# Projection stage of a two-layer hybrid trunk: when the deferred transposes and the splits of the gated outputs are written

## The chip, the cores and the metric

One NeuronCore of a Trainium2 chip runs the whole program in one launch. The metric is the device time in microseconds (us), the median of several executions. Engines are named as in the profile: PE (TensorE, with PEld for its weight loads), DVE (VectorE), ACT (ScalarE), POOL (GpSimd) and SP (SyncE, which issues most DMAs).

## The reference

Two identical layers work on 512 latent tokens and 128 context tokens of width 1024. The context tokens read themselves, the latent tokens read the context cache and all latent tokens.

```
h = rmsnorm(x) * (1 + sc1) + sh1
lru_x, lru_g, gq, gk, gv, dq, dk, dv = split(h @ w_in)      # 256,256,512,128,128,256,256,256 columns
lru_out = gelu(lru_g) * (forward scan + backward scan of the gated recurrence on conv4(lru_x))
gqa_out = softmax attention, 8 query heads on 2 key heads, per-head rmsnorm of q and k, 2-D rotary
d_out   = rmsnorm(softmax(q1 k1) v - lam * softmax(q2 k2) v), 4 heads
x = x + g1 * (concat(lru_out, gqa_out, d_out) @ w_out)
h = rmsnorm(x) * (1 + sc2) + sh2
x = x + g2 * ((silu(g) * a) @ w_down),   a, g = split(conv3(h @ w_up))
```

After the second layer comes one more rmsnorm. The keys, values and scan states of the context tokens are outputs as well.

## The kernel before, in words

Every large product is done in three passes of float32r matmuls: each operand is split into a rounded high part and the rest, and `mm3` (L342 to L346) adds high x high, high x low and low x high. A weight block of 128x1024 comes by a DMA on SP's queue, ACT writes its high part (L329) and DVE its low part (L330).

A layer has these stages in PE's order. The LRU columns m = 0, 1 come first, then three projection groups (`proj_group`, L604): gq, then gk, gv and dq together (`evac_kvdq`), then dk and dv (`evac_dkdv`). Each group has four steps c over the five token tiles, and a tile's result leaves PSUM in the last of them. Then come the LRU's gate columns m = 2, 3 (L1121 to L1125), `wait("a")`, a change of the PSUM pools (`psum_mode(3, 2)`, L1127), attention, the output projection (`out_proj`) and the ConvFFN (`ffn`).

Under the matmuls of the projection stage lies a lot of small work that belongs to attention: norms of the heads, rotary, rounding to high and low parts, and transposes on PE. One such stack for queries: POOL rounds (`s2b`), DVE subtracts (`s3`), PE transposes four blocks (`s4`, tile qT, L844), ACT copies twice. For grouped keys it is `k_stack` (tile kT), for differential keys `d_stack` and `d_stack_flow` (tile dT, whose result DVE copies, L914). The context block has its own small attention: `ctx_stage` (scores cS), `ctx_norm` (DVE), `ctx_T` (transposes cPTp).

Every engine runs its instructions in the order in which the program writes them, and this order comes from a small planner that runs while the program is written, `Flow`. It has a clock `now`. After each pair of k blocks the loops call `fl.step(ns)` with the time that they take the pair to need on PE. Work that has to come later is queued with `fl.add(delay, fn, dve, need)` and written at the first step whose time is past its due time. So a delay of 5000 means a place in program order some steps later, and an instruction written too early waits on its engine with everything behind it. `dve` is the time that `fn` will need on DVE: `fl.dve` is the planner's DVE clock, it moves by these times and by `fl.busy`, and work that has such a time is held back while this clock is over 1500 ns (`slack`) ahead of `now`. `need` names a resource: there are two "st" slots for all stacks. Some functions move `now` themselves, for their own transposes (`fl.now += 230`).

```
def add(self, delay, fn, dve=0.0, need=None):
    self.seq += 1
    self.items.append([self.now + delay, self.seq, fn, dve, need])
```

The gated LRU outputs are made in `lru_in` for m = 2, 3: ACT writes gelu, 800 later DVE multiplies (`mul`, L686), 800 later `mix_out` takes one of 22 buffers of the pool "halves", ACT rounds into it (L639), and DVE writes the rest 800 after that (L640). h itself lies in eight buffers of the same pool.

Between stages, `norm_pipe(t)` turns a finished token tile into h. `a`, 1250 after the tile's last residual, writes the sum of squares on ACT, the root and the two scaled halves xn on POOL (L543). `b`, 4000 (NP[1]) after that, writes eight transposes on PE (tile nT, L549) and the modulation on DVE and ACT. `hi` and `lo` follow 950 and 1700 later. It runs in the last token loops of `tok_products`, where a tile has four pairs of k blocks in the output projection and three in the last part of the FFN. During attention a second planner (`Plan`) sets the order and steps `Flow` by 20 ns.

Of the kernel before, what the change touches and what calls it, by code (L numbers as in the profile page):

```python
# [34 lines left out]
CX = (3000, 6500, 4000, 3000, 6000, 12000, 8000)  # L35
# [10 lines left out]
DT = 1500  # L46
# [8 lines left out]
class Flow:  # L55
# [7 lines left out]
    def add(self, delay, fn, dve=0.0, need=None):  # L63
        self.seq += 1
        self.items.append([self.now + delay, self.seq, fn, dve, need])

# [146 lines left out]
def hybrid_kernel(ctx: ExitStack, tc: tile.TileContext, i, o):  # L213
# [100 lines left out]
    def split_next():  # L314
        if pos[1] >= len(parts):
            return
        n, kind, b = parts[pos[1]]
        pos[1] += 1
        load_to(n)
        if kind == "a":  # L320
            split_done.append(n)
            return
        raw = raws[n][:, :, b * 128:b * 128 + 128] if kind == "c" else raws[n][:, 2 * b:2 * b + 2, :]
        if kind == "h":
            wh, wl = (half(nm, F32R)[:, 0:1024].rearrange("p (a b) -> p a b", a=2) for nm in ("wh", "wl"))
        else:
            wh = whp.tile(list(raw.shape), F32R, tag="wh", name="wh")
            wl = wlp.tile(list(raw.shape), F32R, tag="wl", name="wl")
        act.activation(out=wh, in_=raw, func=ACTF.Copy)  # L329
        dve.tensor_tensor(out=wl, in0=raw, in1=f32(wh), op=ALU.subtract)  # L330
        fl.busy(1130)
        split_done.append((wh, wl))
        if all(m != n for m, _, _ in parts[pos[1]:pos[1] + 3]):
            load_to(n + 2)
# [256 lines left out]
    def stat_mm(acc, w, hh, hl, c, n0=0, n1=KD):  # L591

        wh, wl = w
        for k in range(n0, n1):
            c0, c1 = (0, acc[2]) if c == 0 else (acc[2], T)
            cs = slice(c0, c1)
            mm3(acc[c][:, 0:c1 - c0], wh[:, k, :], wl[:, k, :],
                hh[k // 2][:, k % 2, cs], hl[k // 2][:, k % 2, cs], k == 0, k == KD - 1)
            if k % 2:
                fl.step(816)  # L600
# [12 lines left out]
    def proj_group(hh, hl, evac):  # L613
        acc = tok_acc("acc")
        for c in range(4):
            wh, wl = weights()
            for t in range(NT):
# [7 lines left out]
                fl.step(1296)  # L625


    def mixer(l, hh, hl, first=None):
# [15 lines left out]
        kr, pending = [], {"t": 0.0, "lru": 2, "a": 17}  # L644

        def lru_in(m, acc):
# [33 lines left out]
            else:  # L680
# [4 lines left out]
                def mul():  # L685
                    dve.tensor_tensor(out=gg, in0=gg, in1=lru["S"][:, c], op=ALU.mult)  # L686
                    fl.add(800, lambda: mix_out(c, gg))
# [15 lines left out]
        def lru_tail(c):  # L703
# [33 lines left out]
            fl.add(LT[0], lambda: s1(0), 1500)  # L737
            fl.add(LT[1], lambda: s1(1), 1500)
            fl.add(LT[2], s2)
            fl.add(LT[3], lambda: s3(0), 1700)  # L740
            fl.add(LT[4], lambda: s3(1), 1700)
# [66 lines left out]
        def evac_gq(t, a):  # L808
# [5 lines left out]
            def s1():  # L814
                got["r"] = head_rstd(n, 8)
                if t < 4:
                    fl.add(GQ[1], s2, 2700)
# [3 lines left out]
            def s2():  # L821
                scale_heads(n, got["r"], 8)
                rope(n, t, rope_t["q"], 8, 64)
                for g in range(2):
                    fl.add(100, lambda g=g: s2b(g), 0, "st")

            def s2b(g):
# [3 lines left out]
                fl.add(GQ[2], lambda: s3(g, st), 350)  # L831

            def s3(g, st):
                hs = slice(4 * g, 4 * g + 4)
                dve.tensor_tensor(out=st[:, :, 1 - g], in0=n3[:, hs], in1=f32(st[:, :, g]), op=ALU.subtract)
                fl.add(GQ[3], lambda: s4(g, st))
# [16 lines left out]
            def c2():  # L853
                scale_heads(n, got["r"], 8)
                dve.tensor_tensor(out=n3, in0=n3, in1=rope_t["qg"].unsqueeze(1).to_broadcast([128, 8, 64]), op=ALU.mult)
                fl.add(2500, c3)
# [10 lines left out]
        def k_stack(kf, c0):  # L867
# [6 lines left out]
            def lo():  # L874
                dve.tensor_tensor(out=st[:, 256:384].rearrange("p (h d) -> p h d", d=64), in0=k3, in1=f32(sh[:, :, 0]),
                                  op=ALU.subtract)
                fl.add(1300, tr)
# [14 lines left out]
            fl.add(2000, lo, 200)  # L892
# [27 lines left out]
        def d_stack_flow(lag, *args):  # L920
            lo, tr, out = d_stack(*args)

            def b():
                lo()
                fl.add(lag, c)
# [10 lines left out]
            fl.add(lag, b, 200)  # L936
# [20 lines left out]
        def evac_kvdq(t, a):  # L957
# [16 lines left out]
            def s1():  # L974
                got["r"] = head_rstd(n, 2)
                fl.add(2500, s2 if t < 4 else c2, 1000, "st" if t < 4 else None)

            def s2():
# [3 lines left out]
                fl.add(500, lambda: rope(dqt[:, t], t, rope_t["dq"], 8, 32), 1300)  # L982

            def c2():
# [5 lines left out]
                fl.add(2000, c3)  # L990
# [14 lines left out]
        def evac_dkdv(t, a):  # L1005
            act.activation(out=dv(t if t < 4 else 5), in_=a[:, 256:512], func=ACTF.Copy)
            if t < 4:
                act.activation(out=dkt[:, t], in_=a[:, 0:256], func=ACTF.Copy)
                fl.add(800, lambda: rope(dkt[:, t], t, rope_t["dk"], 8, 32), 1300)
# [34 lines left out]
        def ctx_stage(n):  # L1044
# [7 lines left out]
            fl.add(CX[2], lambda: ctx_norm(n), 900)  # L1052

        def ctx_norm(n):
# [9 lines left out]
            fl.add(CX[3], lambda: ctx_T(n))  # L1064

        def ctx_T(n):
            P = ctxP[n][0]
# [51 lines left out]
        for args in stack_args(0, "k"):  # L1119
            fl.add(CX[4], lambda args=args: d_stack_flow(1500, *args), 0, "st")  # L1120
# [5 lines left out]
        wait("a")  # L1126
        psum_mode(3, 2)  # L1127
# [163 lines left out]
    def tok_products(nk, stat, done, last=4):  # L1291
# [7 lines left out]
        for c in range((nk - last) // 2):  # L1299
            w = weights()  # L1300
            for t in range(NT):
                mms(t, 2 * c, w)
                mms(t, 2 * c + 1, w)
                fl.step(1296)
        ws = []
        for t in range(NT):
            for k in range(nk - last, nk):
# [4 lines left out]
                if k % 2 and k < nk - 1:  # L1312
                    fl.step(1296)
            done(t, acc(t))
            fl.step(1296)
# [331 lines left out]
```

## Time and profile before

| | |
|---|---|
| median of 3 executions | 1642.95 us (1642.11 to 1643.48) |
| the profiled execution | 1643.37 us, of which the span of its instructions is 1641.6 us |
| mean granted TensorE clock | 0.995 of full speed |
| PE busy | 1594.2 us, 97% of the span |
| DVE, ACT, POOL busy | 945.0, 726.3, 344.8 us |

The span is cut by stages: layer 0's projections lie at 49 to 180 us, layer 1's at 854 to 985 us; norm_pipe runs at 342 to 376, 817 to 850 and 1139 to 1176 us. A wait is listed under the engine that sat idle, with what released it. A busy engine isn't all that counts: PE can be busy at half its clock, so the granted clock of a stretch is read beside its busy time.

### The profile page before, as it was taken

The numbers are of one execution on the slowest core, as the hardware profiler recorded it, in microseconds if no ns is written. First come the engines' busy times: TensorE is split into PE (matmuls) and PEld (weight loads), VectorE is DVE, ScalarE is ACT, GpSimd is POOL, SyncE is SP. The second block draws the span as 40 slices with busy tenths as digits, with TensorE's granted clock in tenths as the row PEclk, the third lists the DMA queues.
The fourth block names the chain that finished last, engine by engine and source line by source line (L and its number), as shares of the span: only waits on it lengthen the run. The fifth ranks groups of instructions, "written<-read, shape, count | busy, mean of one in ns | idle before, by whom it ended". The sixth has DMA issues, their size and how long they took to land. (4 is left out here: it accounts for less than half of the span.)

```text
span 1641.6 us, 25381 instructions
## 1 busy us (share of the span) xinstructions
PE 1594.2 (97%) x10070; PEld 1393.8 (85%) x10070; DVE 945.0 (58%) x1548; ACT 726.3 (44%) x1500; POOL 344.8 (21%) x746
## 2 busy tenths in 40 slices
PE   6999899999999999999999999999999999999998
PEld 4778677789999889999887777777899998899986
DVE  5787777465555434555477777865655553355544
ACT  4745677634333212333247357884433331133331
POOL 5162233122111000110052513420411100011101
PEclk9999999999999999999999999999999999999999
DMA  9222465411313221222212214442112232121212
GB/s 331 69 86 78 142 218 208 156 52 53 102 52 108 98 77 52 78 78 90 90 41 71 75 58 155 136 162 102 52 52 86 69 129 78 52 78 54 101 65 90
DMA packets 99435, 161.04 MB, mean 98 GB/s; under 512 B 10670, under 2 KB 69222, under 8 KB 94196
## 3 DMA queue, kind: packets, MB, share of 16 engines
q1 hardware_dynamic: 98068, 158.00, 28.8%
q8 instruction: 79, 1.29, 0.3%
q0 software_dynamic: 1040, 1.14, 0.2%
q14 instruction: 40, 0.33, 0.1%
q10 hardware_dynamic: 208, 0.28, 0.0%
HBM read 155.95 MB, written 3.44 MB: 97 GB/s over the span
## 5 line engine op out<-in xcount | busy, mean ns | idle before, releaser
L330 DVE TENSOR_TENSOR wl<-raw,wh 128x1024 fp32r<-128x1024 f32 x180 | 219.9, 1227 | 410.1 <-ACT wh L329 409.1
L345 PE MATMUL uacc<-hl,wh 128*128 128x320 f32 (+2 forms) x1408 | 437.4, 311 | 0.8 <-DVE hl L574 0.5
L344 PE MATMUL uacc<-hh,wh 128*128 128x320 f32 (+2 forms) x1408 | 435.9, 310 | 0.0
L346 PE MATMUL uacc<-hh,wl 128*128 128x320 f32 (+2 forms) x1408 | 434.2, 308 | 0.2 <-DVE wl L330 0.2
L329 ACT ACTIVATE wh<-raw 128x1024 fp32r<-128x1024 f32 x180 | 189.6, 1059 | 180.3 <-PE tacc L346 148.6
L346 PEld LDWEIGHTS uacc<-hh,wl 128*128 128x128 f32 x1408 | 265.6, 189 | 0.7 <-DVE wl L330 0.7
L345 PEld LDWEIGHTS uacc<-hl,wh 128*128 128x128 f32 x1408 | 264.5, 188 | 1.7 <-DVE hl L574 1.6
L344 PEld LDWEIGHTS uacc<-hh,wh 128*128 128x128 f32 x1408 | 264.7, 188 | 0.3
L344 PE MATMUL tacc<-wh,g 128*128 128x512 f32 x440 | 174.2, 396 | 0.0
L345 PE MATMUL tacc<-wl,g 128*128 128x512 f32 x440 | 173.8, 395 | 0.0
L346 PE MATMUL tacc<-wh,g 128*128 128x512 f32 x440 | 173.3, 394 | 0.0
L1365 POOL TENSOR_SCALAR ca<-u,fcol 128x642 f32<-128x642 f32 x44 | 39.1, 889 | 416.7 <-issue 243.4
L1158 DVE TENSOR_REDUCE nm<-S 128x1 f32<-128x640 f32 x128 | 102.9, 819 | 31.8 <-PE S L1152 16.8
L1162 ACT ACTIVATE P<-S,nm 128x640 f32<-128x640 f32 x128 | 101.2, 793 | 35.0 <-DVE nm L1158 27.4
L1173 POOL TENSOR_SCALAR P<-P,den 128x640 f32<-128x640 f32 x96 | 78.9, 825 | 177.6 <-DVE den L1167 101.3
L1361 ACT ACTIVATE u<-uacc 128x192 f32<-128x192 f32 (+1 forms) x88 | 29.1, 331 | 183.9 <-PE uacc L346 183.9
L346 PEld LDWEIGHTS tacc<-wh,g 128*128 128x128 f32 x440 | 82.6, 188 | 20.0
L344 PEld LDWEIGHTS tacc<-wh,g 128*128 128x128 f32 x440 | 82.6, 188 | 19.6
L345 PEld LDWEIGHTS tacc<-wl,g 128*128 128x128 f32 x440 | 82.7, 188 | 19.1
L344 PE MATMUL acc<-wh,hh 128*128 128x512 f32 x240 | 97.4, 406 | 0.0
L345 PE MATMUL acc<-wl,hh 128*128 128x512 f32 x240 | 95.9, 399 | 0.0
L346 PE MATMUL acc<-wh,hl 128*128 128x512 f32 x240 | 95.7, 399 | 0.0
(291 smaller groups left out, 2673.2 us busy)
## 6 DMA issues: line engine op xcount, KB each, us to landing
raw<-in_ffn_w_up_dram SPq DMA_DIRECT2D x44, 1024.0 KB, 5.1
raw<-in_ada_w_dram SPq DMA_DIRECT2D x40, 1024.0 KB, 4.9
raw<-in_ffn_w_down_dram SPq DMA_DIRECT2D x20, 1024.0 KB, 5.0
raw<-in_w_in_dram SPq DMA_DIRECT2D x16, 1024.0 KB, 8.4
araw<-in_ada_w_dram SPq DMA_DIRECT2D x16, 512.0 KB, 9.6
raw<-in_w_out_dram SPq DMA_DIRECT2D x8, 1024.0 KB, 5.2
gates<-gate SPq DMA_DIRECT2D x8, 512.0 KB
x<-in_x_sample_dram SPq DMA_DIRECT2D x4, 512.0 KB
```

Of the source, the lines that this page charges most:

```text
L329: act.activation(out=wh, in_=raw, func=ACTF.Copy)
L330: dve.tensor_tensor(out=wl, in0=raw, in1=f32(wh), op=ALU.subtract)
L344: pe.matmul(out, lhsT=lh, rhs=rh, start=start, stop=False)
L345: pe.matmul(out, lhsT=lh, rhs=rl, start=False, stop=False)
L346: pe.matmul(out, lhsT=ll, rhs=rh, start=False, stop=stop)
L1158: dve.tensor_reduce(out=box["nm", c], in_=view(c), op=ALU.max, axis=AX.XY, negate=True)
L1162: act.activation(out=box["P"][c].rearrange("p (a b) -> p a b", a=2), in_=view(c), func=ACTF.Exp, bias=box["nm", c], accum_out=box["den"][: ...
L1173: pool.tensor_scalar(out=P[-1], in0=P[-1], scalar1=den[:, 1 + comps:2 + comps], scalar2=0.0, op0=ALU.mult, op1=ALU.add)
L1361: act.activation(out=u[:, 1 + cut:1 + L], in_=acc[1][:, 0:L - cut], func=ACTF.Copy)
L1365: pool.tensor_scalar(out=out, in0=u[:, 1:1 + n], scalar1=wcol(1), scalar2=wcol(3), op0=ALU.mult, op1=ALU.add)
```

## The change

`Flow` gets a second way to queue work, `then`: its due time is the later of the delay and the planner's DVE clock plus a lag of 400 (200 or 600 at two places). The transposes of the query stacks, key stacks and context blocks, and one rounding, are queued with it. The lengths that the planner takes for steps and for DVE work are changed to others. `mix_out` of a gated LRU output is queued 8000 after its product instead of 800. `ctx_T` is put off while a key tile of the second group is still to be rotated, and the projection stage also waits for the differential key stacks of the first pair of heads (`wait(0)`). The diff, with lines of the same kind left out:

```diff
-CX = (3000, 6500, 4000, 3000, 6000, 12000, 8000)
+CX = (3000, 6500, 4000, 3000, 4500, 12000, 8000)
-DT = 1500
+DT = 1100
...
+    def then(self, delay, fn, dve=0.0, need=None, lag=400.0):
+
+        self.add(max(delay, self.dve - self.now + lag), fn, dve, need)
...
@@ split_next
-        fl.busy(1130)
+        fl.busy(1220)
@@ stat_mm
-                fl.step(816)
+                fl.step(888)
@@ proj_group, tok_products (three places)
-                fl.step(1296)
+                fl.step(1390)
@@ mixer
-        kr, pending = [], {"t": 0.0, "lru": 2, "a": 17}
+        kr, pending = [], {"t": 0.0, "lru": 2, "a": 17, "k": 4}
@@ lru_in
-                    fl.add(800, lambda: mix_out(c, gg))
+                    fl.add(8000, lambda: mix_out(c, gg))
@@ lru_tail
-            fl.add(LT[0], lambda: s1(0), 1500)
+            fl.add(LT[0], lambda: s1(0), 2150)
...
-            fl.add(LT[3], lambda: s3(0), 1700)
+            fl.add(LT[3], lambda: s3(0), 2500)
...
@@ evac_gq
-                    fl.add(GQ[1], s2, 2700)
+                    fl.add(GQ[1], s2, 3500)
-                    fl.add(100, lambda g=g: s2b(g), 0, "st")
+                    fl.then(100, lambda g=g: s2b(g), 0, "st", lag=200.0)
-                fl.add(GQ[2], lambda: s3(g, st), 350)
+                fl.add(GQ[2], lambda: s3(g, st), 420)
-                fl.add(GQ[3], lambda: s4(g, st))
+                fl.then(GQ[3], lambda: s4(g, st))
-                fl.add(2500, c3)
+                fl.then(2500, c3)
@@ k_stack
-                fl.add(1300, tr)
+                fl.then(1300, tr)
-            fl.add(2000, lo, 200)
+            fl.then(2000, lo, 290, lag=600.0)
@@ d_stack_flow
-                fl.add(lag, c)
+                fl.then(lag, c)
-            fl.add(lag, b, 200)
+            fl.add(lag, b, 340)
@@ evac_kvdq
-                fl.add(2500, s2 if t < 4 else c2, 1000, "st" if t < 4 else None)
+                fl.add(2500, s2 if t < 4 else c2, 1400, "st" if t < 4 else None)
                 k_stack(n, t * 128)
+                pending["k"] -= 1
...
-                fl.add(2000, c3)
+                fl.then(2000, c3)
@@ ctx_stage, ctx_norm, ctx_T
-            fl.add(CX[2], lambda: ctx_norm(n), 900)
+            fl.add(CX[2], lambda: ctx_norm(n), 900 if n < 2 else 1600)
-            fl.add(CX[3], lambda: ctx_T(n))
+            fl.then(CX[3], lambda: ctx_T(n))
         def ctx_T(n):
+            if pending["k"]:
+                return fl.add(300, lambda: ctx_T(n))
@@ mixer, after the third group
-            fl.add(CX[4], lambda args=args: d_stack_flow(1500, *args), 0, "st")
+            fl.add(CX[4], lambda args=args: d_stack_flow(900, *args), 0, "st")
...
         wait("a")
+        wait(0)
         psum_mode(3, 2)
```

## Rows read from the trace of the kernel before

**Rows 1.** Page, part 1: busy us, share of the span and instructions of each engine.
```profile
PE 1594.2 (97%) x10070; PEld 1393.8 (85%) x10070; DVE 945.0 (58%) x1548; ACT 726.3 (44%) x1500; POOL 344.8 (21%) x746
```

**Rows 2.** PE's waits, 28 to 195 us: total us, times, longest.
```profile
PE dT L910 <- DVE ds L905: 2.7, 2, 2.5
...
PE qT L844 <- DVE gqs L835: 1.3, 1, 1.3
...
PE cqT L861 <- DVE gqr L855: 0.8, 1, 0.8
```

**Rows 3.** PE's waits, 820 to 1005 us (dT and cqT have the same rows again).
```profile
PE nT L549 <- POOL xn L543: 2.1, 3, 1.3
PE qT L844 <- DVE gqs L835: 1.2, 1, 1.2
```

**Rows 4.** Timelines of ACT, DVE, PE, 168 to 180 us: start, length, [idle before <-releaser].
```profile
170.75 0.74 ACT L639 ACTIVATE mix<-lrug 128x640 fp32r<-128x640 f32 x1 [4.49 <-PE lacc L345]
...
171.52 0.83 DVE L640 TENSOR_TENSOR mix<-lrug,mix 128x640 fp32r<-128x640 f32 x1 [2.69 <-ACT mix L639]
...
172.93 0.48 DVE L905 TENSOR_TENSOR ds<-db,ds 128x128 fp32r<-128x128 f32 x2
...
173.35 0.63 PE L910 MATMUL dT<-identr,ds 128*96 128x128 f32 x4 [2.49 <-DVE ds L905]
...
178.42 0.45 PE L910 MATMUL dT<-identr,ds 128*96 128x128 f32 x4 [0.19 <-DVE ds L905]
...
179.81 0.38 PE L1147 MATMUL S<-kk,qa 128*128 128x320 f32 x1 [0.70 <-DVE dks L914]
```

**Rows 5.** Timeline of PE, 112 to 116 us.
```profile
113.42 0.88 PE L844 MATMUL qT<-identr,gqs 128*128 128x128 f32 x8 [1.26 <-DVE gqs L835]
115.08 1.08 PE L861 MATMUL cqT<-ident,gqr 128*128 128x128 f32 x4 [0.78 <-DVE gqr L855]
```

**Rows 6.** Busy time by stretches of 2 us: length, PE, PEld, DVE, ACT, POOL, then granted clock, DMA share, GB/s.
```profile
114.00:116.00 2.00, 1.22 (x9) 1.08 (x8) 1.96 (x3) 1.40 (x5) 0.00 (x0) 0.79 0.46 143
116.00:118.00 2.00, 2.00 (x6) 1.61 (x6) 0.55 (x3) 0.60 (x1) 1.40 (x4) 0.50 0.00 0
118.00:120.00 2.00, 2.00 (x9) 1.55 (x8) 0.30 (x2) 0.92 (x4) 1.16 (x3) 0.86 0.00 0
```

**Rows 7.** Timelines, 342 to 348 us: end of token tile 0 in the output projection to its transposes.
```profile
342.26 0.40 PE L344 MATMUL tacc<-wh,mix 128*128 128x512 f32 x1
342.46 0.69 DVE L1287 TENSOR_TENSOR res<-tacc,gates 128x512 f32<-128x512 f32 x1 [0.39 <-PE tacc L346]
...
345.79 1.37 POOL L543 TENSOR_SCALAR xn<-x,rs_r 128x512 f32<-128x512 f32 x2
...
347.81 1.04 PE L549 MATMUL nT<-ident,xn 128*128 128x128 f32 x8
```

**Rows 8.** Timelines, 833 to 840 us: last part of the FFN of layer 0.
```profile
834.27 0.68 DVE L1287 TENSOR_TENSOR res<-tacc,gates 128x512 f32<-128x512 f32 x1
...
838.39 0.66 PE L549 MATMUL nT<-ident,xn 128*128 128x128 f32 x4 [1.26 <-POOL xn L543]
...
839.74 0.66 PE L549 MATMUL nT<-ident,xn 128*128 128x128 f32 x4 [0.69 <-POOL xn L543]
```

**Rows 9.** PE's timeline, 155 to 157 us.
```profile
155.51 0.38 PE L882 MATMUL kT<-identr,gks 128*128 128x128 f32 x3
156.42 0.44 PE L1019 MATMUL cdkT<-ident,cdk 128*128 128x128 f32 x2 [0.54 <-ACT cdk L1012]
```

**Rows 10.** Timelines of POOL and DVE: the parts of one differential key stack.
```profile
162.60 0.41 POOL L349 TENSOR_SCALAR ds<-db 128x256 fp32r<-128x256 f32 x1 [1.41 <-DVE db L795]
...
177.32 0.75 DVE L914 CAST dks<-dT 96x256 fp32r<-96x256 f32 x2 [1.02 <-PE dT L910]
```

**Rows 11.** ACT's timeline in the FFN, 431 to 433 us.
```profile
431.79 0.74 ACT L1394 ACTIVATE cg<-cg 128x642 f32<-128x642 f32 x1 [3.07 <-DVE cg L1369]
```

More of the change, by code (lines that the diff above doesn't have):

```diff
@@ L735, in s4 @@
                 pending["lru"] -= 1
-            fl.add(LT[0], lambda: s1(0), 1500)
-            fl.add(LT[1], lambda: s1(1), 1500)
+            fl.add(LT[0], lambda: s1(0), 2150)
+            fl.add(LT[1], lambda: s1(1), 2150)
             fl.add(LT[2], s2)
-            fl.add(LT[3], lambda: s3(0), 1700)
-            fl.add(LT[4], lambda: s3(1), 1700)
+            fl.add(LT[3], lambda: s3(0), 2500)
+            fl.add(LT[4], lambda: s3(1), 2500)
             fl.add(LT[5], s4, 700)
@@ L981, in s2 @@
                 k_stack(n, t * 128)
-                fl.add(500, lambda: rope(dqt[:, t], t, rope_t["dq"], 8, 32), 1300)
+                pending["k"] -= 1
+                fl.add(500, lambda: rope(dqt[:, t], t, rope_t["dq"], 8, 32), 1500)
             def c2():
@@ L1008, in evac_dkdv @@
                 act.activation(out=dkt[:, t], in_=a[:, 0:256], func=ACTF.Copy)
-                fl.add(800, lambda: rope(dkt[:, t], t, rope_t["dk"], 8, 32), 1300)
+                fl.add(800, lambda: rope(dkt[:, t], t, rope_t["dk"], 8, 32), 1600)
             else:
@@ L1303, in tok_products @@
                 mms(t, 2 * c + 1, w)
-                fl.step(1296)
+                fl.step(1390)
         ws = []
@@ L1312, in tok_products @@
                 if k % 2 and k < nk - 1:
-                    fl.step(1296)
+                    fl.step(1390)
             done(t, acc(t))
-            fl.step(1296)
+            fl.step(1390)
             if pos[1] < len(parts) and parts[pos[1]][1] == "h" and t >= 1:
```

## The prediction

> **What bounds the kernel now.** I read the busy times first: PE has work for 1594.2 of 1641.6 us, every other engine for 58% or less [rows 1]. So the time is PE's own work plus what PE waits, and a change of order can only win where PE waits or runs slowly. The list of PE's waits, taken for the two projection stages, shows where. In layer 0 they are the differential key transposes dT (2.7 us), the query transposes qT (1.3) and the context queries cqT (0.8) [rows 2], in layer 1 the same three, with 1.2 for qT [rows 3] and the other two as in layer 0. Third I read the timelines around the two largest gaps, to see what the released instruction had stood behind.
>
> The 2.49 us before dT end with DVE's subtraction at 172.93. That stood behind the split of a gated output, for which DVE sat idle 2.69 us until 171.52, because ACT's half of it started only at 170.75, when PE had let go of a buffer of h [rows 4]. So PE waits for DVE, DVE for ACT, ACT for PE. The gap before qT is of another kind: DVE was busy all along (1.96 of 2.00 us next to it [rows 6]), and the planner had written the transposes ahead of the place where DVE was through with their input [rows 5].
>
> Last I read the granted clock in 2 us stretches. After the qT and cqT gaps it is at 1.2 GHz, half of 2.4: the three stretches show 0.79, 0.50 and 0.86 [rows 6], so PE loses 0.42 + 1.00 + 0.28 = 1.7 us of work there. The same happens after the dT gap (0.80, 0.50, 0.85) and at both places of layer 1 (0.68, 0.50, 0.97 and 0.68, 0.50, 0.96): four falls, 1.7 us each.
>
> **The change part by part.** All terms are against the profiled execution (1643.37 us, 1.8 of it outside the span); the median is 0.4 lower and I shift by that at the end.
>
> **Gated outputs 8000 later.** This moves one ACT instruction (0.74) and one DVE instruction (0.83) per column block [rows 4], no DMA. A pair of k blocks in m = 3 is one step of 888, so the first block's split lands about nine steps later, near the end of m = 3, when the first buffers of h are free; the second lands some 8 us into attention. The chain of three waits is gone then, and with it 2.49 + 0.19 us of idle per layer [rows 4] and one fall of the clock, 1.7: 2 x 4.4 = 8.8 us. Nobody waits for these outputs before the output projection. In attention, ACT and DVE get 1.5 and 1.7 us more per layer under PE's work; the cover is that they are busy 58% and 44% of the span [rows 1], and if it is missing at the very start the price is 0.74 per layer.
>
> **Transposes after DVE's clock.** What moves is, per query stack, eight or four transposes and their ACT copies; per key stack three transposes and three copies; for the context four transposes, two copies and two output DMAs on POOL's queue, which only round-offs stand behind. PE fills the place with matmuls that it has anyway. The waits at qT and cqT are worth 1.26 + 0.78 in layer 0 and 1.2 + 0.8 in layer 1 [rows 2, 3, 5], with two falls of the clock: 2.0 + 2.0 + 3.4 = 7.4 us. The planner's DVE clock does not count the copies of dT (0.75 per stack [rows 10]) or the score maxima, so I don't take all: 0.8 us per layer stays as a short wait, as large as the cqT wait of today. The first two parts together are 8.8 + 7.4 - 1.6 = 14.6 us gained, of at most 16.2 and at least 0.
>
> The price of a transpose: context keys cdkT wait 0.54 us for ACT today, with three kT transposes (0.38) in front of them [rows 9]. If those are moved, that cover goes and PE waits 0.3 longer: +0.6 for two layers (0 to 0.7).
>
> **Waits and holds.** `wait(0)` costs nothing where all five dT groups are already before the first attention score, and they are: the fifth starts at 178.42 [rows 4], and attention's first scores at 179.81. Putting off `ctx_T` delays four transposes and one ACT copy that nobody needs before attention.
>
> **Step lengths, everywhere.** 816 to 888 and 1296 to 1390 also shift every delay outside the projections, and here I find a cost. `norm_pipe` queues its transposes 4000 after its first part. Three steps were 3888, so four were needed; now three are 4170 and enough. In the output projection a token tile has four pairs, PE spends 347.81 - 342.26 = 5.55 us on four [rows 7], so the transposes come 1.39 us earlier, 4.2 us after the tile's end. Their input isn't ready then: the first half of xn ends at 345.79 + 0.68 = 346.47, the second at 347.16, which is 4.2 and 4.9 after 342.26 [rows 7]. With a signal's delay the first four transposes wait 0.1, the other four, which follow within 0.45, 0.25. That is 0.4 us for tile 0. For tiles 1 to 3 I take 0.6, since modulation work of the tile before now lies next to the chain. Four tiles make 2.2, two output projections 4.4 (0 where DVE and POOL are relieved by the new order, at most the whole 1.39 per tile, 11.1).
>
> In the last part of layer 0's FFN a tile has three pairs, and the old distance alternates between four and three; one tile with three waits 1.26 + 0.69 = 1.95, because its residual starts at 834.27, over 2 us late, behind `lo` of the tile before, which waits for POOL [rows 8]. With the new steps every tile has three. POOL still rounds tile t-1 behind xn of tile t, so the lateness repeats: about 0.4, 0.3, 1.3 and 1.3 = 3.3 against 1.95, that is +1.3 (-2 to +3.6).
>
> In the FFN pairs the Silu is now due after 6 steps and not 7. Today ACT reaches it 3.07 us before its input is there [rows 11] and PE doesn't mind, as weights are split a tile ahead: 0.
>
> **Sum.** -14.6 + 0.6 + 4.4 + 1.3 = -8.3 us: 1635.1 for a run like the profiled one, 1634.6 for the median.
>
> One rule of the Trainium skill speaks against a part of this. Its page "TensorE: Matmul & The Clock Gate", Part 1 (the HAM clock gate), says that for modelling, the ramp penalty is under 1% of a typical kernel span and is not to be fitted. By that I would leave the clock out, the gain would be 6.8 us less and the median 1641.4. The rows price the half clock directly (0.50 over whole stretches in which PE was busy), so they decide.
>
> **The rivals.** A measurement of this kernel tells apart about 0.2%, 3.3 us.
> 1. *The norm chain keeps up.* Rounding of the tile before now precedes xn on POOL in the output projection, so the residual is never late, and the nT waits come out near today's. For it: today's tile 1 in the FFN has three pairs and no wait. Against it: tile 0's 4.9 us chain has nothing before it that could go. Then -14.6 + 0.6 = -14.0: 1629.
> 2. *The planner's DVE clock is not DVE's.* It counts neither waits for POOL and ACT nor the copies; where DVE has no idle time (1.96 of 2.00 us [rows 6]) any error adds up, so the transposes there still meet an unfinished input a little later, and only the gated outputs' 8.8 come in. In this case half of the change doesn't do what it says. -8.8 + 6.3 = -2.5: 1640.5.
> 3. *The waits shrink, the 1.2 GHz stretches stay,* since what is left of the gaps at the same places is enough for the fall. Idle time of 9.4 less 1.6 against 6.3: 1641.4. The page's rule above comes out at the same place.
> 4. *Slower: the key stacks slip past the last projection matmul.* `then` only delays, each stack holds one of two slots for longer, and `wait("a")` and `wait(0)` have no matmuls to lie under. If three of the five differential stacks are left at that point, two rounds of POOL 0.41, DVE 0.24, PE 0.45, DVE 0.75 [rows 4, 10] and the signals between them, about 2.2 us each, lie bare, and the clock falls once: 6.1 per layer. -8.3 + 12.2 = +3.9: 1646.8. It decides from three stacks on; with one or two the result stays faster. Against it: the start is 1500 earlier (4500), both lags are 900 and the 16 steps now count 14208, not 13056.
>
> **How the numbers follow.** Forecast 0.51, with its own range of 1630 to 1639 (its waits and nT terms half or double); rival 1 0.17, rival 2 0.17, rival 3 0.07, rival 4 0.08. The range of 1628.5 to 1642 leaves out the better half of rival 1 and rival 4. Faster by over 0.2% means under 1639.7: nearly all of the forecast, rival 1 and some of rivals 2 and 3, 0.73. Within 0.2%: the rest of these, 0.21. Slower: 0.06, most of rival 4.
>
> **What would show it.** Right: PE's waits in the two projection stages have no dT row, qT and cqT together under 1 us per layer, the granted clock is 1.00 from 108 to 124 and from 168 to 180 us, ACT's row for the gated split has no long wait; the nT waits, 2.1 us at layer 0's end [rows 3] and under 0.5 at the other two boundaries, have grown to some 8 in all, with waits of 0.3 to 1.4 at most tiles of all three boundaries. Wrong: nT stays as it is (rival 1), qT or cqT waits reappear at other times (rival 2), clock under 1.00 without a long wait before it (rival 3), or dT and S rows with over 1.5 us at 175 to 185 us and bare waits ahead of attention (rival 4). A wait in attention or inside the FFN pairs, which I cost at nothing, would be a term that I missed.

## The result and the profile after

The changed kernel takes **1651.81 us** (median; 1650.68 to 1652.88), beside 1642.68 (1642.11 to 1643.48) for the kernel before on the same chip: a ratio of 1.0055, 95% interval 1.0038 to 1.0073. It is slower by 9 us where I forecast 8 us faster, and it lies outside the range. The profiled execution took 1652.67 us with a span of 1650.9.

Part 1 of the page answers to [rows 1]. PE is busy 2.2 us longer in a span that is 9.3 longer, so the loss is mostly waiting:

```profile
PE 1596.4 (97%) x10070; PEld 1390.4 (84%) x10070; DVE 945.0 (57%) x1548; ACT 725.5 (44%) x1500; POOL 345.0 (21%) x746
```

PE's waits over the whole span (total us, times, longest) show that the two lists of waits have little in common:

```profile
...
PE S L1155 <- ACT lrug L687: 4.6, 2, 2.3
PE nT L553 <- POOL xn L547: 4.5, 12, 0.7
...
PE S L1155 <- ACT P L1170: 3.9, 5, 1.5
PE ckT L1002 <- DVE kd L993: 3.5, 2, 1.7
...
PE dT L914 <- DVE ds L909: 2.2, 2, 1.1
...
PE tacc L349 <- DVE wl L334: 1.5, 2, 0.8
PE tacc L348 <- ACT wh L333: 1.5, 2, 0.8
PE cdkT L1024 <- ACT cdk L1017: 1.5, 2, 0.7
```

The qT and cqT rows of [rows 2, 3] are gone and the 2.5 us of dT with them. In their place stand waits that before had no row (S for `lrug`, the Gelu of the LRU's gate, ckT for `kd`, the output projection's matmuls for their weights) or a smaller one. The table says where in the span this costs time. It is read from PE's timeline of the two profiled executions, from the first matmul of one kind to the first of the next, both named in the first column.

| stretch (layer 0 / layer 1), us | before | after | difference |
|---|---|---|---|
| projections, first `acc` to first `lacc` | 107.23 / 104.75 | 106.81 / 102.86 | -0.4 / -1.9 |
| last projection, first `lacc` to first score S | 23.19 / 23.32 | 22.99 / 22.98 | -0.2 / -0.3 |
| attention, first S to first `tacc` | 126.38 / 117.98 | 127.73 / 119.69 | +1.4 / +1.7 |
| output projection, first `tacc` to first `uacc` | 61.68 / 62.08 | 66.04 / 66.19 | +4.4 / +4.1 |
| end of the FFN, first `tacc` to next `lacc` | 75.59 / - | 76.53 / - | +0.9 |

Two things are to be seen: the output projections, which the change touches only by a step length, lose 8.5 us, and the projections, which it was made for, win almost nothing.

**The output projection.** ACT's timeline in the changed kernel, 340 to 343 us:

```profile
340.71 0.63 ACT L533 ACTIVATE sqj<-x 128x512 f32<-128x512 f32 x1 [0.66 <-DVE x L1296]
341.25 0.18 ACT L533 ACTIVATION_READ_ACCUMULATOR sqj<-x 128x1 f32 x1
341.34 1.99 ACT L333 ACTIVATE wh<-raw 128x1024 fp32r<-128x1024 f32 x2
```

and PE's there:

```profile
342.44 0.50 PE L348 MATMUL tacc<-wh,mix 128*128 128x512 f32 x1 [0.75 <-ACT wh L333]
343.70 0.50 PE L349 MATMUL tacc<-wl,mix 128*128 128x512 f32 x1 [0.76 <-DVE wl L334]
...
349.24 1.32 PE L553 MATMUL nT<-ident,xn 128*128 128x128 f32 x8
356.43 1.32 PE L553 MATMUL nT<-ident,xn 128*128 128x128 f32 x8 [0.30 <-POOL xn L547]
```

The sum of squares `sqj` is queued 1300 behind its tile. That was two steps of 1296 and is one of 1390, so ACT meets it before DVE's residual x is there, and the two halves of the next weight split (wh), queued behind it, start at 341.34; PE waits 0.75 and 0.76 us for them. The nT transposes now wait at each of the four following tiles (1.3 us in all, 0.30 in the row), and eight of them take 1.32 us where [rows 7] show 1.04.

**Ahead of the first score.** ACT's timeline in the changed kernel, 177 to 181 us:

```profile
177.06 0.38 ACT L1080 ACTIVATE vb<-cPTp 128x256 f32<-128x256 f32 x1 [3.24 <-PE cPTp L1078]
177.45 1.28 ACT L687 ACT_TABLE_LOAD   x1
178.75 0.77 ACT L687 ACTIVATE lrug<-lacc 128x320 f32<-128x320 f32 x2
179.40 0.74 ACT L643 ACTIVATE mix<-lrug 128x640 fp32r<-128x640 f32 x1
```

and PE's first score:

```profile
179.56 0.41 PE L1155 MATMUL S<-kk,qa 128*128 128x320 f32 x1 [2.29 <-ACT lrug L687]
```

The last context transposes are now written ahead of the last column block's Gelu, where before they stood behind it. ACT runs in order: its copy of cPTp waits 3.24 us for PE to come to these transposes, and the Gelu's table load, which had been done by then under PE's matmuls, stands behind the copy. Load (1.28) and Gelu (0.77) lie bare, and only then does PE get the buffer that its first score needs. The keys are late as well. [Rows 9] show the last kT transposes before, at 155.51; in the changed kernel PE's last ones are these:

```profile
168.23 0.37 PE L886 MATMUL kT<-identr,gks 128*128 128x128 f32 x3
```

The Trainium skill ("ScalarE: Activation LUTs", What ACT_TABLE_LOAD costs) puts 1380 ns of draining on top of a load of some 1283 ns. The rows agree with the load (1.28 us), but show no such gap on either side of it: the copy before the load ends at 177.44, the Gelu starts at 178.75.

**At ckT.** DVE's timeline in the changed kernel, 118 to 126 us:

```profile
118.48 1.15 DVE L805 TENSOR_REDUCE hss<-hsq 128x2 f32<-128x128 f32 x5 [2.04 <-ACT hsq L803]
120.30 1.23 DVE L334 TENSOR_TENSOR wl<-raw,wh 128x1024 fp32r<-128x1024 f32 x1 [0.67 <-ACT wh L333]
124.49 0.49 DVE L810 TENSOR_TENSOR kr<-kr,rs_r 128x128 f32<-128x128 f32 x1 [2.97 <-POOL rs_r L360]
125.01 0.37 DVE L991 TENSOR_TENSOR kr<-kr,rope 128x128 f32<-128x128 f32 x1
125.48 0.29 DVE L993 COPY kd<-kr 128x256 f32<-128x256 f32 x1
```

All five head norms of the key group come in one block at 118.48. POOL then works off five norm chains, from 118.92 to 124.45 us, DVE sits idle 2.97 us for the last one, and PE's ckT waits 1.74 us for the copy `kd`. That copy is no later than it was before, as DVE's and PE's timelines of the kernel before show:

```profile
125.50 0.29 DVE L988 COPY kd<-kr 128x256 f32<-128x256 f32 x1
127.65 0.27 PE L997 MATMUL ckT<-ident,kd 128*128 128x128 f32 x1
```

It is PE that comes sooner: counted from the first `acc` it is free for ckT after 74.4 us and not 78.3, and in layer 1 after 72.0 and not 75.8, while `kd` is ready only 0.4 us sooner in both. So the 3.8 us per layer that the gaps at qT and cqT had cost did come back, and 1.7 of them were lost again at the next place, where the norm chain had been 1.9 us ahead of PE. The granted clock behind that gap, by stretches of 2 us (columns as in [rows 6]):

```profile
124.00:126.00 2.00, 0.26 (x2) 0.11 (x2) 1.37 (x4) 0.00 (x0) 1.57 (x4) 1.00 1.08 379
126.00:128.00 2.00, 2.00 (x15) 1.80 (x16) 0.45 (x2) 1.41 (x6) 1.98 (x5) 0.87 0.32 97
128.00:130.00 2.00, 2.00 (x6) 1.57 (x5) 0.68 (x1) 1.29 (x3) 0.76 (x3) 0.50 0.00 0
130.00:132.00 2.00, 2.00 (x8) 1.59 (x8) 1.22 (x3) 0.00 (x0) 0.00 (x0) 0.78 0.00 0
```

The four falls to 1.2 GHz of before are gone from the two projection stages, and this is the one new one. In layer 1 the same wait of 1.7 us has none behind it.

### The profile page after: what moved, and what is told of

Its sections match the earlier page's. It is cut to its first block, busy times and chain, and to the rows that moved or that the text cites. A ratio compares the mean times of both kernels' runs of the same rounds, so it can differ in the third digit from the quotient of the medians.

```text
span 1650.9 us, 25393 instructions
## 1 busy us (share of the span) xinstructions
PE 1596.4 (97%) x10070; PEld 1390.4 (84%) x10070; DVE 945.0 (57%) x1548; ACT 725.5 (44%) x1500; POOL 345.0 (21%) x746
## 4 chain that ended last, share of the span: by engine, by line
PE 82%; DVE 6%; ACT 4%; POOL 3%; issue 2%; DMA 1%; SPq 1%; POOLq 0%; DVEq 0%; ACTq 0%
PE uacc L348 12%; PE uacc L349 12%; PE uacc L350 12%; PE tacc L349 7%; PE tacc L348 7%; PE tacc L350 7%; PE PV L1213 3%; PE PT L1190 3%; PE acc L349 2%; PE acc L350 2%; PE acc L348 2%; PE ada L491 2%; PE S L1160 1%; PE S L1155 1%; POOL xn L547 1%
```

## The experiments

Fifteen kernels ran, each beside the kernel before on the same chip (its median was 1641.75, 1641.87, 1641.54 and 1641.93 us in the four groups). Ratios are to that, with the 95% interval.

### Step lengths or projections?

`e1_tok1296`: the changed kernel with the step of the token products (output projection and FFN, three places) as it was.

```diff
-                fl.step(1390)
+                fl.step(1296)
```

> The changed kernel with the step of the token products (output projection, FFN down) back at 1296; everything else of the change stays. Theory A (the loss lies in the step lengths there: one pair earlier for the norm transposes, one step earlier for the sums of squares that stand before the weight splits): the two output projections and the last part of the FFN give back 4.3 + 4.1 + 1, so about 1642 to 1643 us, as before the change, and the nT waits are near 2.5 us. Rival B (the loss there is handed on from attention or from the longer projection stage, by weights that come late): the stretch from the output projection to the first up products stays at 66 us, time 1650 or more. Rival C (the loss lies in the projection and attention stages): under 3 us are given back.

Measured: 1640.17 us, ratio 0.9992 (0.9984 to 1.0001). Taking back the length alone gives 11.6 us (10.3 by the ratios: the kernel before read 0.9 us less on this chip), and the output projections are back at 61.6 and 61.9 us. What is left of the change, all of it in the projections and what follows from them, is worth 1.6 us and can't be told from nothing.

`e2_before_tok1390`: the other way round, the kernel before with only those steps lengthened.

> The kernel before with only the three steps of the token products at 1390. Theory A: slower by 9 to 10 us, about 1652, with waits of tacc for weights (0.8 + 0.8 us per layer) and some 4.5 us at nT. Rivals B and C: within 2 us of before.

Measured: 1649.70 us, 1.0051 (1.0038 to 1.0064): 8.0 us slower by one number in the planner, with no instruction added. That is less than 11.6, but the intervals of the two (6.2 to 10.5, and 7 to 13 from the ratios of e1 and of the changed kernel) overlap. Its output projections take 66.1 and 66.3 us, as in the changed kernel.

`e3_np5000` and `e4_sumsq1500` keep the step of 1390 in the changed kernel and put one delay each back to the pair in which it came before:

```diff
-NP = (1250, 4000, 950, 1700)
+NP = (1250, 5000, 950, 1700)
...
-fl.add(1300, lambda hf=hf: sumsq(t, hf))
+fl.add(1500, lambda hf=hf: sumsq(t, hf))
```

> The changed kernel with the norm transposes queued 5000 and not 4000 after their first part, so that they take four pairs again. Theory A: the part of the norm transposes comes back, 2.7 us per output projection and about 1 in the FFN, 6 us, so 1645.5; the weight waits of tacc (1.5 us per layer) stay. If the norm transposes cost nothing net (their waits would only move): 1651 to 1652.

> The changed kernel with the sums of squares of the first half queued 1500 and not 1300 after a tile's residual, so that they take two steps again. Theory A: the weight waits of tacc go, 1.4 us per layer, so 1649; the nT waits stay. If the weight splits were late for another reason: 1651 to 1652 with the tacc waits in place.

Measured: 1644.82 us with the later transposes (ratio 1.0023, 1.0014 to 1.0031), so 7.0 less than the changed kernel; 1647.46 us with the later sums (1.0041, 1.0028 to 1.0054), 4.4 less. Together 11.4, so within the noise the two delays are the whole of e1's 11.6. The stretches of the output projections say so more closely: the later transposes take 2.8 and 2.6 us off them, the later sums 1.7 and 1.7, together 4.4 and 4.3, where 4.4 and 4.1 were lost.

### The gated outputs

`e7_before_mix8000`: the kernel before, with only the gated outputs later. `e8_mix800`: the kernel of e1, with only these as they were.

```diff
-                    fl.add(800, lambda: mix_out(c, gg))
+                    fl.add(8000, lambda: mix_out(c, gg))
```

> The kernel before with only the gated outputs 8000 later (mix_out); steps, DVE lengths and transposes as they were. Theory A (the prediction's term holds by itself): the dT wait of 2.49 us and the stretch of half clock behind it go in both layers, 8.8 us less, 1633; the qT and cqT waits and their two falls stay. Theory B (the split only changes its neighbours: it lands on the end of the projection and pushes the lrug product or a score's inputs back): the dT wait goes, but a wait of 1.5 us or more at the first scores (S) takes its place, 1637 to 1642.

> The changed kernel with token-product steps of 1296 (1640.17 us) and with the gated outputs back at 800, so that the steps of 888, the DVE lengths and the transposes behind DVE's clock are left. Theory A (the two parts are separate, as the prediction summed them): the dT wait of 2.5 us and its fall of the clock come back in both layers, about 8 us more, 1648. Theory B (behind DVE's clock, the dT stacks lie elsewhere and no longer behind the split): within 3 us of 1640.

Measured: e7 takes 1635.28 us, 0.9959 (0.9947 to 0.9971), 6.6 less than before. The stretch from the first `lacc` to the first score goes from 23.19 to 19.22 us and from 23.32 to 19.18, 4.0 and 4.1 less against the 4.4 that I took. Attention then gets 1.2 and 1.4 us longer. e8, where the same line is turned the other way, takes 1645.3 us, 1.0022 (1.0013 to 1.0030), so within the changed kernel the same edit is worth 5.1. The gated outputs do what they should in both. It follows that the rest of the projection's change, by the difference of e1 and e7, costs 4.9 us where I had 5.2 gained (7.4 less 1.6 and 0.6).

### Are the short gaps worth what I took?

`e9_cq_late`: e7 with the context queries' transposes one step later, by a fixed delay.

```diff
-                fl.add(2500, c3)
+                fl.add(3400, c3)
```

> The kernel before with the gated outputs 8000 later (1635.28 us) and with the context queries' transposes (cqT) 3400 instead of 2500 behind their product; the query transposes stay. Theory A (the prediction's price of a short gap: idle time plus the fall of the clock that qT and cqT share): the cqT wait of 0.78 us goes, the qT wait of 1.2 stays, and with one gap left the stretch of half clock behind it stays out too, 2 x 2.5 = 5 us less, 1630. Theory B (a single qT gap is still enough for the fall): 2 x 0.8 = 1.6 us less, 1633.7. Theory C (the wait comes back at ckT, which waits for PE's place and the same POOL chain): 1635.

Measured: 1631.9 us, 0.9947 (0.9933 to 0.9961), the fastest of the study and faster than both kernels. In both layers the projections take 2.4 us less than in e7 (104.71 against 107.11, 102.28 against 104.72), though the idle time that went is 0.78. The stretches of 2 us behind the place, in e7:

```profile
114.00:116.00 2.00, 1.22 (x12) 1.08 (x11) 1.97 (x3) 1.41 (x5) 0.00 (x0) 1.00 0.59 184
116.00:118.00 2.00, 2.00 (x8) 1.53 (x6) 0.82 (x3) 0.60 (x1) 1.13 (x3) 0.58 0.00 0
118.00:120.00 2.00, 2.00 (x7) 1.57 (x6) 0.81 (x3) 0.92 (x4) 1.67 (x6) 0.57 0.00 0
```

and in e9_cq_late:

```profile
114.00:116.00 2.00, 2.00 (x14) 1.69 (x13) 1.97 (x4) 1.60 (x7) 0.00 (x0) 1.00 0.40 125
116.00:118.00 2.00, 2.00 (x11) 1.65 (x10) 0.91 (x5) 1.57 (x7) 1.48 (x4) 1.00 0.00 0
118.00:120.00 2.00, 2.00 (x10) 1.61 (x9) 1.10 (x4) 1.52 (x7) 1.67 (x5) 1.00 0.00 0
```

The second gap gone, the clock stays at 2.4 GHz, although the first is still there, as PE's timeline of e9_cq_late shows:

```profile
113.33 0.88 PE L844 MATMUL qT<-identr,gqs 128*128 128x128 f32 x8 [1.25 <-DVE gqs L835]
...
115.51 0.60 PE L861 MATMUL cqT<-ident,gqr 128*128 128x128 f32 x4
```

So 0.78 us of waiting cost 2.4, as theory A had it for this stage. The whole gained 3.4 us and not its 5: attention and the FFN of layer 0 took some 0.8 back in the profiled runs. The Trainium skill ("TensorE: Matmul & The Clock Gate", Part 1, the HAM clock gate) puts the ramp penalty at under 1% of a typical kernel span and advises against fitting it to a count of cold matmuls. Here it is 1.6 us at each of two places, 0.2% of the span, which agrees with its figure; but it is as large as the differences that are to be told apart, so it belongs in the sum.

`e13_cq_late_mix1_40000`: e9 with the second gated output deep in attention.

```diff
-                    fl.add(8000, lambda: mix_out(c, gg))
+                    fl.add(40000 if c else 8000, lambda: mix_out(c, gg))
```

> As e9_cq_late, with the second gated output 40000 instead of 8000 behind its product, so that its two instructions (0.73 on ACT, 0.82 on DVE) lie deep in attention and not among the first probabilities. Theory A (the 1.2 and 1.4 us by which attention grew are PE waiting for probabilities behind that split): 2 us less than e9_cq_late. Theory B (attention starts at the same DVE and ACT work either way, and what the projection gave up comes back there): within 1 us of e9_cq_late.

Measured: 1632.07 us, 0.9949 (0.9935 to 0.9963), and attention takes 128.22 and 119.17 us against 127.93 and 119.33. For the whole it doesn't matter where the second split stands in attention. What the first one costs can be read in part. DVE's timeline, in the kernel before:

```profile
180.72 0.82 DVE L1158 TENSOR_REDUCE nm<-S 128x1 f32<-128x640 f32 x1
181.47 0.82 DVE L640 TENSOR_TENSOR mix<-lrug,mix 128x640 fp32r<-128x640 f32 x1
```

and in e7:

```profile
176.50 0.81 DVE L640 TENSOR_TENSOR mix<-lrug,mix 128x640 fp32r<-128x640 f32 x1
...
177.44 2.28 DVE L1158 TENSOR_REDUCE nm<-S 128x1 f32<-128x640 f32 x3
```

In e7 DVE's half of a split stands ahead of the first maximum of the scores (`nm`), which starts 1.45 us after the first score (175.99) and not 0.91 (179.81); in layer 1 it is 1.44 and not 0.92. ACT's first probabilities come 0.5 us later by this, and PE's scores behind them too (4.57 us after the first score, 4.05 before). The rest of the 1.2 and 1.4 us stays open.

### Which part of the rest costs the 4.9 us?

`e10_steps888`: e7 with the projection's step and the weight split's length alone.

```diff
-                fl.step(816)
+                fl.step(888)
...
-        fl.busy(1130)
+        fl.busy(1220)
```

> The kernel before with the gated outputs 8000 later (1635.28 us) and of the rest of the change only the projection's step of 888 instead of 816 and the weight split's 1220 instead of 1130; no transpose behind DVE's clock, no other length. Theory A (the loss of 4.9 us against the changed kernel with token steps of 1296, 1640.17, comes with the transposes behind DVE's clock): within 2 us of 1635.3. Theory B (the steps alone push the key stacks and the norm chains to the end): 1638 or more, with the waits of the changed kernel (ckT 1.7, S for lrug 2.3).

Measured: 1636.9 us, 0.9974 (0.9966 to 0.9983), 1.6 more than e7: not these, as theory A had it. One wait replaced another on the way: cqT has no row any more, and kT waits 2.1 us for ACT's context probabilities.

`e12_then_only`: the kernel of e1 with DVE's lengths and the step of 816 as they were (the token groups of the projections keep 1390, L629), so that the transposes behind DVE's clock, the stacks' starts, the holds and the gated outputs are left.

```diff
-                fl.step(888)
+                fl.step(816)
...
-                    fl.add(GQ[1], s2, 3500)
+                    fl.add(GQ[1], s2, 2700)
...
```

> The changed kernel with token-product and projection steps as before for token products (1296, four places with the projection's own at 1390) and stat steps at 816, and with DVE's lengths in the planner as they were; so of the projection's change the transposes behind DVE's clock, the stacks' starts, the two holds and the gated outputs are left. Theory A (transposes held behind DVE's clock cost by themselves, since they hold the two stack slots longer): 1639 to 1642, with S waits over 1.5 us. Theory B (the longer lengths are what holds DVE's work back; with the short ones the transposes move little): 1634 to 1637, with the waits of the kernel before (qT 1.2, cqT 0.8) and no ckT wait.

Measured: 1653.15 us, 1.0079 (1.0064 to 1.0094), 13 more than e1. Neither theory holds. I read it so: with a clock that runs short, `then` writes the transposes too early again, and other instructions behind them. PE's waits of this kernel, 28 to 195 us:

```profile
PE qT L848 <- DVE gqs L839: 2.6, 1, 2.6
PE acc L349 <- DVE wl L334: 2.2, 2, 1.7
PE kT L886 <- POOL gks L353: 2.2, 1, 2.2
```

So `then` with the short lengths is worse than with the long ones, and the two can't be weighed one by one. The lengths without `then` were not tried on the chip, nor the query transposes put off by a fixed delay.

### The new waits, one at a time

`e6_c3_late`: the kernel of e1, with the context keys' transposes two steps later. `e5_end`: the kernel of e1, with ctx_T of tile 3 behind the Gelu and the gated outputs at 12000.

```diff
-                fl.then(2000, c3)
+                fl.then(4000, c3)
...
-            fl.then(CX[3], lambda: ctx_T(n))
+            fl.then(CX[3] + (3000 if n == 3 else 0), lambda: ctx_T(n))
-                    fl.add(8000, lambda: mix_out(c, gg))
+                    fl.add(12000, lambda: mix_out(c, gg))
```

> The changed kernel with token-product steps of 1296 (1640.17 us) and with the context keys' last part (c3, which writes ckT) 4000 instead of 2000 behind its product. Theory A (DVE's clock in the planner misses its wait for POOL's rs_r chain, so ckT is written 1.7 us early, and that is what PE pays): the ckT wait of 1.7 us goes in both layers and layer 0's stretch of half clock with it, 2 x 1.74 + 1.7 = 5.2 us less, 1635. Theory B (whatever stands next on PE waits for the same late chain): the wait moves to cdkT, dT or kT with over 1 us, and the time stays within 2 us of 1640.

> The changed kernel with token-product steps of 1296 (1640.17 us), with the last context transposes (ctx_T of tile 3) 3000 later and the gated outputs at 12000 instead of 8000, so that ACT's copy of cPTp and the split stand behind the Gelu and the lrug product. Theory A (order on ACT at the end of the projection makes the S wait): S waits for lrug 0.7 us per layer instead of 2.3, 3 us less, 1637. Theory B (the first scores wait for the last stacks anyway): the S row names another releaser (ds, P or vb) with the same 2 us, and the time stays at 1640.

Measured: e6 takes 1645.02 us, 1.0017 (1.0008 to 1.0026), 4.9 more than e1; e5_end takes 1642.51 us, 1.0009 (0.9999 to 1.0020), no better than e1. The waits moved as theory B has it in both, though e6 loses more than the 2 us that it allows. In e6 the ckT wait is gone and a qT stands in its place; PE's timeline:

```profile
135.42 0.72 PE L848 MATMUL qT<-identr,gqs 128*128 128x128 f32 x4 [2.64 <-ACT cP L1044]
```

In e5_end the wait for `lrug` is gone, and the first score waits for the last key stack instead:

```profile
177.23 0.39 PE L1155 MATMUL S<-kk,qa 128*128 128x320 f32 x1 [1.81 <-DVE dks L918]
```

Moving the instruction that waits moves the wait. What is late lies ahead of it.

### What is late, and why

`e14_kvnorm`: the kernel of e1; the head norms of the key group are no longer held back while the planner's DVE clock is ahead.

```diff
-            fl.add(600, s1, 250)
+            fl.add(600, s1)
```

`e15_st3`: the kernel of e1 with a third slot for stacks. `e16_kvnorm_st3`: both.

```diff
-    fl.free["st"] = 2
+    fl.free["st"] = 3
```

> The changed kernel with token-product steps of 1296 (1640.17 us), with the head norms of the key group (s1 in evac_kvdq) no longer held back while the planner's DVE clock is ahead (their length is 0 instead of 250). Theory A (the longer DVE lengths hold these five short reductions back to the end of their group, POOL then does five norm chains in a row, and ckT is written in the middle of them): the ckT wait of 1.7 us goes in both layers without another in its place, 3.5 us less, 1636.7, and the key stacks come earlier too. Theory B (the transposes are written where PE has no cover whatever is late): ckT or its neighbour still waits 1.5 us or more, 1640.

> The changed kernel with token-product steps of 1296 (1640.17 us), with three stack slots (st) instead of two. Theory A (transposes held behind DVE's clock hold the two slots longer, so the key and differential stacks slip to the end, where the dT wait of 1.1 and the S wait of 2.3 us lie bare): with a third slot the stretch from the first column block of the last projection to the first score, 22.99 us, comes down towards the 19.2 of e7, 2 x 3 us less, 1634. Theory B (DVE's own work is late, not the slots): the stretch stays within 1 us of 22.99 and the time within 2 us of 1640.

> Both edits of e14_kvnorm and e15_st3. If both causes hold and are separate, ckT and the bare waits before attention go together: 1631 to 1633, about what e9_cq_late gives. If DVE's late work is the only cause, no better than e14_kvnorm alone.

Measured: e14 takes **1634.67 us**, 0.9960 (0.9948 to 0.9972), 5.5 less than e1, more than theory A's 3.5. DVE's timeline of e14, to be read against that of the changed kernel above:

```profile
115.13 0.47 DVE L805 TENSOR_REDUCE hss<-hsq 128x2 f32<-128x128 f32 x2
...
116.84 0.28 DVE L805 TENSOR_REDUCE hss<-hsq 128x2 f32<-128x128 f32 x1
...
117.85 0.29 DVE L805 TENSOR_REDUCE hss<-hsq 128x2 f32<-128x128 f32 x1
119.25 0.29 DVE L805 TENSOR_REDUCE hss<-hsq 128x2 f32<-128x128 f32 x1 [1.11 <-ACT hsq L803]
...
122.29 0.49 DVE L810 TENSOR_TENSOR kr<-kr,rs_r 128x128 f32<-128x128 f32 x1 [0.87 <-POOL rs_r L360]
122.81 0.37 DVE L991 TENSOR_TENSOR kr<-kr,rope 128x128 f32<-128x128 f32 x1
123.21 0.29 DVE L993 COPY kd<-kr 128x256 f32<-128x256 f32 x1
```

The norms come as their inputs do, POOL's last chain is through 2.2 us earlier (DVE goes on at 122.29, not 124.49), and ckT, at 124.84, has no wait. In e12, which has `then` and the old lengths, the five norms come one at a time as well (at 123.00, 123.64, 126.13, 127.12 and 128.52 us on DVE's timeline), and in e10, with the step of 888 but `fl.add` and the old DVE lengths of the norms, only three stand together (116.08). So the block comes with the longer DVE lengths and not with `then` or the step. The last kT of e14 comes at 162.69 on PE's timeline:

```profile
162.69 0.37 PE L886 MATMUL kT<-identr,gks 128*128 128x128 f32 x3
```

With the keys earlier the order at the end is another, too: the copy of cPTp is behind the Gelu again, the score waits 0.7 us for it and not 2.3 for `lrug`, and the stretch ahead of the score goes from 22.99 to 21.36 us.

e15 takes 1650.01 us, 1.0051 (1.0038 to 1.0064), and e16 1650.76, 1.0055 (1.0043 to 1.0067): 10 more than e1, the stretch ahead of the first score longer (23.59 in e15), the dT wait up to 2.0. So two slots are not what makes the stacks late; with a third one the order comes out worse.

## Why the prediction was wrong

**What held.** The dT wait with its fall of the clock went: 4.0 and 4.1 us ahead of the first score by e7 for 4.4 each. The price of the qT and cqT gaps held too: both left no row in the changed kernel, PE is at ckT 3.9 and 3.8 us sooner for the 3.7 per layer of the prediction, and e9 shows 2.4 us per layer for the part that it removes, where idle time and half clock made 2.5. The four falls to 1.2 GHz are gone, with one new one at another place. Rival 3 falls by this, and with it the sum that leaves the clock out.

**First failed step: what the lengths do besides.** "The planner's DVE clock does not count the copies of dT ... so I don't take all: 0.8 us per layer stays as a short wait." I costed the longer lengths only as what the transposes wait for. The same clock also holds back every DVE item with a length while it is over 1500 ahead. The five head norms of the key group were held so until they came in one block (118.48), and POOL's chains, which the clock doesn't count, came behind them in a row, and the key stacks after these. PE, being 3.8 us sooner, ran into them. Instead of 0.8 us per layer, PE waits 1.7 at ckT, 1.1 at dT, 2.3 at the first score (0.7 before), 0.8 more for P, and some 1.0 more at kT, cdkT and for weights (wl).

By e1 the projections keep 1.6 us of 14.0. Its stretches, against those before, say where the 12.4 went: the projections gain 1.9 per layer for 2.6 (3.7 less 0.8 and 0.3), the last projection 0.2 and 0.3 for 4.4, because the keys are late (nine kT and four cPTp transposes more than before lie in it, beside the waits at dT and S), and attention takes 1.2 and 1.6 more for nothing. e14 shows this cause for its part: with that hold taken away 5.5 us come back. The rest of the projection's change then gains 0.6 us over e7 where I had 5.2. Rival 2 named the clock that isn't DVE's, but expected its error at qT and cqT, where the clock served, and put the loss at no more than the transposes' own term.

The cover in attention failed as well. "In attention, ACT and DVE get 1.5 and 1.7 us more per layer under PE's work" was put at nothing, or 0.74 per layer without cover; e7 shows 1.2 and 1.4, of which 0.5 is DVE's half of the first split ahead of the first maximum.

**Second: the place of the last context copy.** "Putting off `ctx_T` delays four transposes and one ACT copy that nobody needs before attention." True of the data, but I didn't place the copy in ACT's order. Tile 3's copy came ahead of the Gelu, and the first score waits 2.3 us for the Gelu's result. The hold is not what put it there: the last key tile is rotated on DVE by 161 us, and the norm that queues tile 3's `ctx_T` comes at 173.78. With the steps alone (e10), with the hold and `then` but the old lengths (e12, where the score waits 0.5 us for that copy) and with the norms released (e14) the copy stands behind the Gelu, so the place is an accident of the planner's times. With that place mended alone (e5_end) the score waits 1.8 us for the late keys in its stead; with the keys earlier 0.7 are left (e14).

**Third: the step of 1390.** I saw that a delay of 4000 now takes three steps and priced its nT waits at 4.4 + 1.3 = 5.7. By the stretches it is 2.8 + 2.6 in the output projections and 0.9 at the FFN's end, some 6.4, so about right (7.0 by the median of e3, whose FFN end is 0.8 us shorter than before the change). The sign that I gave, nT waits of some 8 us, failed: their row has 4.5, and the rest is transposes that wait between one another. I missed that 1300 is crossed as well: two steps of 1296, one of 1390. That is 4.4 us by e4's median and 3.3 by the stretches, and the rows show weight splits waiting on ACT behind a sum whose input is not there.

**The sum.** Projections -1.6 for -14.0, step lengths +11.6 for +5.7: +10.0, where I had -8.3; measured +9.1, the difference being that between the two chips' kernels before. Two thirds of the error (12.4 of 18.3) lie in the projections. The chance of 0.06 for slower was wrong in kind, too: rival 4 asked for stacks beyond the last matmul, while the loss that decides the sign was my own term for the step lengths, at twice its size by the second delay that I missed.

What stays open: all but 0.5 us of the 1.2 to 1.7 by which attention is longer, what brought tile 3's copy ahead of the Gelu, and what `then` is worth without the longer lengths.

## What to carry to other kernels

When a planner's length is changed, list every delay that it divides and every item that it holds back: a delay just above a multiple of the old step (1300 over 1296, 4000 over three of them) jumps to another place, and an item held by a busy clock may be short, cheap and at the head of the longest chain. When a wait is taken away, follow the late input to where it begins before moving the instruction that waits; e6 and e5_end only moved the wait, e14 moved its cause. When PE is to come sooner, ask of the next thing that it meets how far ahead its inputs are (1.9 us for ckT, and PE came 3.8 sooner). Two fixed delays at places that the trace had shown (e9) gave 9.6 us; the rule for all transposes, without the token steps, gave 1.6 (e1).

## What the runs showed of the hardware

Two gaps of PE near each other (1.18 and 0.78 us, in e7) were followed by 1.2 GHz, and one of 1.25 in the same place was not (e9). A wait of 1.7 us at ckT was followed by it in layer 0 of the changed kernel and not in layer 1, nor in either layer of e1. The wait of 2.3 us at the first score was followed by it in layer 0 of e1 and in neither layer of the changed kernel. So a gap's length alone doesn't tell whether the clock falls; a forecast should hold both cases, 1.6 to 1.7 us apart for each place.
